# Differences for a seven-product matrix multiplication read back from DRAM as whole rows, and a modulation row moved to PSUM with four loads in flight

## The chip, the core and the metric

The kernel runs on one core of one Trainium2 chip. The metric is the device time of one execution in microseconds (us). Five engines work in parallel, each through its own instruction queue in order: TensorE (PE, with its weight loads as PEld), VectorE (DVE), ScalarE (ACT), GpSimd (POOL) and SyncE (SP), which in this kernel issues every DMA. [...]

## The reference

One layer of a hybrid diffusion backbone over 1024 latent tokens of width 1024, with 256 context tokens. The change touches the two places marked below.

```python
mod_l = (jax.nn.silu(c) @ w_mod[i] + b_mod[i])            # rows 2..5 are "modulation()" in the kernel
sh1, sc1, g1, sh2, sc2, g2 = jnp.split(mod_l, 6, axis=-1)
hl = modulate(rmsnorm(xl, norm1_w[i]), sh1, sc1)          # the normed rows
# token mixer: hl @ w_in is split into SSD input, z, Fourier input, gMLP u and v, and gate logits
g = jax.nn.sigmoid(gate_logits)                           # gate_logits = hl @ w_in[:, OFF_GATE:]
m = g0 * (y_ssd @ w_ssd_o) + g1 * (y_fft @ w_fft_o) + g2 * (y_gmlp @ w_gmlp_o)
xl = xl + g1 * (m @ w_out)
hl2 = modulate(rmsnorm(xl, norm2_w[i]), sh2, sc2)
xl = xl + g2 * conv_ffn(hl2, ...)
return rmsnorm(xl, final_norm_w)
```

## The kernel before

**Number format.** All products are of fp32 data, each operand carried as a high part (fp32r) and a low part that holds the rest: three matmuls (high x high, low x high, high x low) make one product. `hh[k]` and `hl[k]` (k = 0..7, 128 rows x 1024 tokens each) are the high and low part of the modulated, normed latent rows, made in the opening: VectorE scales `xk` in place, ScalarE adds the shift and writes `hh[k]` (L265), VectorE writes `hl[k]` (L266).

**Stages, in order of time.** Opening with the modulation of the first norm (0 to 92 us); projections and the SSD scan (to 545); the v, Fourier and z tiles (to 684); the gates (to 925); the branch products, the output projection and the MLP. A v tile is a projection, a GELU, eight transposes, and a product with `wsT` into `psgm`, which VectorE reads at L750. A z tile (`z_tile`, numbers 4 to 7 here) is 48 matmuls into a PSUM tile `psz`, a tanh on ScalarE (`th`, L649) and a read by VectorE (L650) that frees the PSUM tile. The PSUM pool of the z tiles (two tiles of 1024 columns) is released behind the last z tile, and the gates take its banks in tiles of 512 columns.

**Gates.** 24 blocks of gate logits are made two by two with seven products in place of eight: `gate_unit` and `unit_steps`, with weight combinations from `weight_tools` (`raw` loads `A11`..`A22`, `s_` adds or subtracts, `put` splits into high and low part, L844 to L850) and with operand combinations of four blocks of the normed rows: b11 and b12 are the token halves of rows k, b21 and b22 those of rows k + 4. Needed are t1 = b12 - b11, t2 = b22 - t1, t3 = b22 - b12 and t4 = b21 - b11 - t3, for k = 0..3, each split again into a high and a low part (`split`, L166 and L167). Before, each difference is made from the parts: the low parts subtracted on GpSimd (L1164), the high parts on VectorE (L1166, L1173), then a sum (L1167, L1174), and for t4 one subtraction more (L1180). The tiles come from pool `wx`: tag `rw` with five buffers, which the weight loads `A..` use too, and tag `ws` with three.

**Modulation.** `modulation()` makes the four later modulation rows on VectorE: 64 tensor_tensor_reduce (L1211) of 128 x 512, each on a piece of `w_mod` that SyncE loads into one of the two halves of a tile (`ctanh`), times the SiLU row `crow`, which lies in SBUF. One pair of them is put behind each addition of a gate unit.

**Order.** The code is written in program order; a list scheduler orders each engine's queue by a model of its own, and priorities (`tc.high_priority`) and `tc.issue_after` steer it.

Of the kernel before, what the change touches and what calls it, by code (L numbers as in the profile page):

```python
# [32 lines left out]
def hybrid_block_kernel(ctx: ExitStack, tc: tile.TileContext, a, dbg=None):  # L33
    nc = tc.nc
    V, S, G, PE, SY = nc.vector, nc.scalar, nc.gpsimd, nc.tensor, nc.sync
# [11 lines left out]
    dram = pool("dram", space=bass.MemoryType.DRAM)  # L47
# [4 lines left out]
    def ps_small(name, tag="c"):  # L52
        return pss.tile([P, 512], F32, tag=tag, name=name)
# [105 lines left out]
    def f32(t):  # L159
        return t.bitcast(F32)  # L160
# [34 lines left out]
    for k in range(KT):  # L195
        xk = xT[k // 4][:, k % 4, :]
# [3 lines left out]
        q = s2.tile([P, L], F32, tag="CT", name=f"sqx{k}")  # L200
# [33 lines left out]
    def mod_rows(k):  # L234
# [10 lines left out]
        with tc.high_priority(offset=CHAIN):  # L245
            V.tensor_copy(mrow[k % 2], crow[k % 2])

    hh = [None] * KT
    hl = [None] * KT
    for k in range(KT):  # L250
        mod_rows(k)
        with tc.high_priority(offset=CHAIN):
            for s_ in range(2):
                o = 4 * k + 2 * s_
                PE.matmul(psmod[:, o:o + 2], mrow[k % 2][:, s_ * P:(s_ + 1) * P], sel, start=True, stop=True)
            V.tensor_tensor(mods[:, k], psmod[:, 4 * k:4 * k + 4].rearrange("p (s v) -> p s v", s=2),
                            bc(bmod[:, k:k + 9:8].unsqueeze(2), [P, 2, 2]), op=ALU.add)
            V.scalar_tensor_tensor(mods[:, k, 1], mods[:, k, 1], 1.0, bc(n1w[:, k:k + 1], [P, 2]),
                                   op0=ALU.add, op1=ALU.mult)
        shl, Al, shc, Ac = mods[:, k, 0, 0:1], mods[:, k, 1, 0:1], mods[:, k, 0, 1:2], mods[:, k, 1, 1:2]  # L260
        hh[k] = hpool.tile([P, L], F32R, tag="h", name=f"hh{k}")
        hl[k] = hpool.tile([P, L], F32R, tag="h", name=f"hl{k}")
        xk = xT[k // 4][:, k % 4, :]
        V.scalar_tensor_tensor(xk, xk, Al, rbx, op0=ALU.mult, op1=ALU.mult)
        last_op["hh"] = S.activation(hh[k], xk, AF.Identity, bias=shl)  # L265
        V.scalar_tensor_tensor(hl[k], xk, shl, f32(hh[k]), op0=ALU.add, op1=ALU.subtract)  # L266
        ck = ctxT[k // 4][:, k % 4, :]
        V.scalar_tensor_tensor(ck, ck, Ac, rbc, op0=ALU.mult, op1=ALU.mult)
        S.activation(hch[:, k, :], ck, AF.Identity, bias=shc)
# [373 lines left out]
    def z_tile(g, i, qz):  # L643
        t = 4 * g + i
        wt = win(T_Z + t, f"wz{t}")
        ps = ps_big(f"psz{t}")
        mm3(halves(ps), wt, hx, KT)
        th = tpool.tile([P, L], F32, tag="acc", name=f"th{t}")
        S.activation(th, ps, AF.Tanh, scale=0.5)  # L649
        V.scalar_tensor_tensor(th, th, 1.0, ps, op0=ALU.add, op1=ALU.mult)  # L650
        yv = yacc[g][:, i, :]
        V.tensor_tensor(yv, yv, th, op=ALU.mult)
        if i == 0:
            S.activation(qz, yv, AF.Square)
            return
        q = tpool.tile([P, L], F32, tag="tmp", name=f"yq{t}", bufs=1)
        S.activation(q, yv, AF.Square)
        (G if i % 2 else V).tensor_tensor(qz, qz, q, op=ALU.add)
        if i == 3:
            tok_sums(psq[g], qz, NCH)  # L660
# [49 lines left out]
    for u in (0, 1, 4, 2, 3):  # L710
# [3 lines left out]
        for par, (tt, c0, n) in enumerate(((tpf, 0, NE), (tmf, NE, NO))):  # L714
            ps = ps_small(f"psU{u}{par}", ("c", "c2")[par])
# [52 lines left out]
    HB = 512  # L768
    HS = (slice(0, HB), slice(HB, L))
    ORDER = (1, 6, 5, 7, 2, 3, 4)  # L770
    wx = pool("wx", bufs=2, side="left")
# [381 lines left out]
            h, l = xt[2 * j + k // 2]  # L1153
            Bh[p].append((h[:, k % 2, :], l[:, k % 2, :]))
    for k in range(4):
        b11, b12 = (hh[k][:, HS[0]], hl[k][:, HS[0]]), (hh[k][:, HS[1]], hl[k][:, HS[1]])
        b21, b22 = (hh[k + 4][:, HS[0]], hl[k + 4][:, HS[0]]), (hh[k + 4][:, HS[1]], hl[k + 4][:, HS[1]])

        def tmp(q, tag="rw", n_=5):
            return wx.tile([P, HB], F32, tag=tag, name=f"H{q}{k}", bufs=n_)  # L1160

        def diff(q, x, y):
            o, t = tmp(q), tmp(f"d{q}", "ws", 3)
            G.tensor_tensor(t, f32(x[1]), f32(y[1]), op=ALU.subtract)  # L1164
            with tc.issue_after(last_op["F"].ins):
                V.tensor_tensor(o, f32(x[0]), f32(y[0]), op=ALU.subtract)  # L1166
            V.tensor_tensor(o, o, t, op=ALU.add)  # L1167
            return o

        t1 = diff(1, b12, b11)  # L1170
        t2 = tmp(2)
        with tc.issue_after(last_op["F"].ins):
            V.tensor_tensor(t2, f32(b22[0]), t1, op=ALU.subtract)  # L1173
        V.tensor_tensor(t2, t2, f32(b22[1]), op=ALU.add)  # L1174
        split(t2, *Bh[6][k], V)
        split(t1, *Bh[5][k], G)
        t3 = diff(3, b22, b12)
        split(t3, *Bh[7][k], G)
        t4 = diff(4, b21, b11)
        V.tensor_tensor(t4, t4, t3, op=ALU.subtract)  # L1180
        split(t4, *Bh[4][k], V)

    def gate_unit(b, d, md):
        def consume(r, h, src, spare):
# [14 lines left out]
    def modulation():  # L1199
        cr = tpool.tile([P, D], F32, tag="zz", name="crow", bufs=1)  # L1200
        SY.dma_start(cr, a["crow"].partition_broadcast(P))
        ct = tpool.tile([P, D], F32, tag="tmp", name="ctanh", bufs=1)
        S.activation(ct, cr, AF.Tanh, scale=0.5)
        V.scalar_tensor_tensor(cr, ct, 1.0, cr, op0=ALU.add, op1=ALU.mult)
        wm = ct.rearrange("p (i c) -> p i c", i=2)
        for i in range(2):
            SY.dma_start(wm[:, i], a["wmod1"][0, 0, :, HS[i]])
        for b in range(4):
            for k in range(KT):
                for i in range(2):  # L1210
                    V.tensor_tensor_reduce(out=wm[:, i], in0=wm[:, i], in1=cr[:, HS[i]], scale=0.5, scalar=0.0,  # L1211
                                           op0=ALU.mult, op1=ALU.add, accum_out=mod2[:, i, b, k:k + 1])
                    n_ = b * KT + k + 1
                    if n_ < 4 * KT:
                        SY.dma_start(wm[:, i], a["wmod1"][n_ // KT, n_ % KT, :, HS[i]])
                yield

    y_norm(1, ("y", "y"))
# [518 lines left out]
```

## Time and profile before

| | us |
|---|---|
| median of three runs | 1914.47 (1911.53 to 1917.52) |
| the profiled execution, own time | 1915.69 |
| its span, first to last instruction | 1913.9 |
| PE busy | 1754.1 |
| DVE busy | 1413.0 |
| ACT busy | 849.0 |
| POOL busy | 890.3 |

The profiled execution is 1.2 us above the median of the runs, and its own time 1.8 us above its span. "Busy" is the sum of an engine's instruction times; the idle time in front of an instruction is shown with the engine or DMA that ended it.

### The profile page before, as it was taken

To read this page: it belongs to the slowest core of one execution; us is meant where nothing else is said; L and a number is where in the kernel's file an instruction comes from. 1 tells how busy PE (TensorE), PEld (TensorE's weight loads), DVE (VectorE), ACT (ScalarE), POOL (GpSimd) and SP (SyncE) were. 2 spreads that over 40 slices of the span, in tenths; PEclk is the share of its full clock that TensorE was granted. 3 is DMA by queue.
4 is the path that set the end of the run, shared out by engine and by line. 5 is a ranking of instruction groups with operands and counts; after the bars stand their busy time and mean duration, and the time that the engine had idled before them with its cause. 6 is when DMAs were issued, how large, how long until landed. Compare 5 with 4: busy or idle time off the path is not lost. (4 is left out here: it accounts for less than half of the span.)

```text
span 1913.9 us, 23639 instructions
## 1 busy us (share of the span) xinstructions
PE 1754.1 (92%) x8148; PEld 1409.3 (74%) x8148; DVE 1413.0 (74%) x2002; ACT 849.0 (44%) x1472; POOL 890.3 (47%) x591
## 2 busy tenths in 40 slices
PE   4899998897989879999799999889999999899888
PEld 3688776675668768777687888678888888677677
DVE  7786576786675854666848645899888888968896
ACT  5444355564442334434434234445455545533433
POOL 3222255456542654544655855534343333544543
PEclk9899999999999989999999999899999999899998
DMA  8012365654453124666246463123223224653532
GB/s 331 6 64 67 124 194 145 159 155 116 160 178 105 39 88 165 209 203 217 89 130 207 142 233 131 53 84 109 94 98 133 89 97 167 203 180 113 167 109 89
DMA packets 144608, 260.36 MB, mean 136 GB/s; under 512 B 15452, under 2 KB 56284, under 8 KB 143080
## 3 DMA queue, kind: packets, MB, share of 16 engines
q1 hardware_dynamic: 144488, 258.86, 41.5%
q8 instruction: 64, 1.05, 0.2%
q14 instruction: 56, 0.46, 0.1%
HBM read 205.71 MB, written 53.10 MB: 135 GB/s over the span
## 5 line engine op out<-in xcount | busy, mean ns | idle before, releaser
L1211 DVE CUSTOM_DVE_ANT_0 ctanh<-ctanh,crow 128x512 f32<-128x512 f32 x64 | 57.0, 897 | 41.6 <-DMA ctanh<-in_wmod_dram 41.4
L286 DVE SCALAR_TENSOR_TENSOR acc<-psx,convw,acc 128x1023 f32<-128x1023 f32 (+1 forms) x48 | 61.4, 1279 | 20.0 <-ACT acc L282 19.6
L555 DVE SCALAR_TENSOR_TENSOR rf<-rs,ncuml,rf 128x128 f32<-128x128 f32 x128 | 47.2, 416 | 31.4 <-ACT rf L554 28.9
L1264 POOL TENSOR_TENSOR pwo<-rwo,pwo 128x512 fp32r<-128x512 f32 x32 | 46.9, 1475 | 46.5 <-ACT pwo L1263 43.0
L850 POOL TENSOR_TENSOR w1up<-A11up,w1up 128x512 fp32r<-128x512 f32 x20 | 27.1, 1356 | 88.8 <-ACT w1up L849 79.6
L561 POOL TENSOR_TENSOR rf<-rf,G 128x512 f32<-128x512 f32 x32 | 46.1, 1443 | 45.8 <-DVE G L558 35.5
L850 POOL TENSOR_TENSOR w7up<-S3up,w7up 128x512 fp32r<-128x512 f32 x20 | 29.4, 1472 | 79.9 <-ACT w7up L849 46.2
L558 DVE SCALAR_TENSOR_TENSOR G<-cbm,dtl,G 128x128 f32<-128x128 f32 x128 | 58.6, 517 | 6.0 <-ACT G L557 6.0
L1553 DVE SCALAR_TENSOR_TENSOR xf<-Yd,g,xf 128x512 f32<-128x512 f32 x64 | 46.9, 743 | 11.6 <-PE Yd L860 11.5
L554 ACT ACTIVATE rf<-rf,ncuml 128x128 f32<-128x128 f32 x128 | 41.2, 393 | 31.2 <-DMA rf<-Rd 31.1
L166 ACT ACTIVATE gh<-gr 128x1024 fp32r<-128x1024 f32 (+1 forms) x36 | 37.1, 1034 | 37.5 <-DMA gr<-Gd 36.0
L157 PE MATMUL pso<-mh,pwo 128*128 128x512 f32 x128 | 50.2, 392 | 0.0
L153 PE MATMUL pso<-mh,pwo 128*128 128x512 f32 x128 | 49.8, 390 | 0.0
L155 PE MATMUL pso<-ml,pwo 128*128 128x512 f32 x128 | 49.8, 389 | 0.0
L510 DVE TENSOR_TENSOR scr<-po,ro 128x512 f32<-128x512 f32 x32 | 21.8, 685 | 34.8 <-ACT ro L497 34.6
L497 ACT ACTIVATE ro<-ro 128x512 f32<-128x512 f32 x32 | 20.1, 629 | 58.9 <-DMA ro<-Rd 58.5
L520 PE MATMUL pS<-scr,Bt 128*128 128x512 f32 x56 | 32.1, 658 | 14.4 <-DVE scr L510 13.2
L1469 DVE TENSOR_TENSOR gt<-gt,aa 128x512 f32<-128x512 f32 x44 | 42.9, 974 | 0.1
L557 ACT ACTIVATE G<-cbm,dtl 128x128 f32<-128x128 f32 x128 | 39.7, 391 | 6.4 <-DVE cbm L545 6.4
L850 POOL TENSOR_TENSOR w4up<-A22up,w4up 128x512 fp32r<-128x512 f32 x20 | 31.2, 1559 | 21.2 <-ACT w4up L849 21.2
L1466 ACT ACTIVATE ft<-aa 128x512 f32<-128x512 f32 x44 | 27.8, 631 | 29.5 <-DVE aa L1448 29.5
L522 POOL TENSOR_TENSOR st<-st,etl 128x512 f32<-128x512 f32 x24 | 26.6, 1108 | 29.3 <-DVE st L524 29.3
(1292 smaller groups left out, 6670.4 us busy)
## 6 DMA issues: line engine op xcount, KB each, us to landing
gr<-Gd SPq DMA_DIRECT2D x70, 256.0 KB, 3.4
ctanh<-in_wmod_dram SPq DMA_DIRECT2D x64, 256.0 KB, 3.4
Gd<-gt SPq DMA_DIRECT2D x10, 1536.0 KB, 5.7
wm<-in_wmod_dram SPq DMA_DIRECT2D x16, 512.0 KB, 9.8
ro<-Rd SPq DMA_DIRECT2D x64, 128.0 KB, 3.2
rf<-Rd SPq DMA_DIRECT2D x32, 256.0 KB, 4.6
rs<-Rd SPq DMA_DIRECT2D x32, 256.0 KB, 3.7
sg<-Sg SPq DMA_DIRECT2D x16, 512.0 KB, 3.6
```

Of the source, the lines that this page charges most:

```text
L153: PE.matmul(o, wh[:, k, :], xh[:, sl], start=st, stop=False)
L155: PE.matmul(o, wh[:, k, :], xl[:, sl], start=False, stop=False)
L157: last_op["mm"] = PE.matmul(o, wl[:, k, :], xh[:, sl], start=False, stop=sp)
L286: V.scalar_tensor_tensor(acc[:, lo:hi], ps[:, lo + o:hi + o], cw[:, t, j:j + 1], acc[:, lo:hi], op0=ALU.mult, op1=ALU.add)
L555: V.scalar_tensor_tensor(E[:, h, :], rs[:, h, :], ncum[:, c, 16 + f:17 + f], E[:, h, :], op0=ALU.add, op1=ALU.min)
L558: V.scalar_tensor_tensor(Gm[:, h, :], cbm[:, 1, :], dtl[:, c, 16 + f:17 + f], Gm[:, h, :], op0=ALU.mult, op1=ALU.add)
L561: G.tensor_tensor(E, E, Gm, op=ALU.mult)
L850: (V if p in on_v else G).tensor_tensor(t[:, 1, :], ap, f32(t)[:, 0, :], op=ALU.subtract)
L1211: V.tensor_tensor_reduce(out=wm[:, i], in0=wm[:, i], in1=cr[:, HS[i]], scale=0.5, scalar=0.0, op0=ALU.mult, op1=ALU.add, accum_out=mod2[:, ...
L1264: G.tensor_tensor(t[:, 1, :], raw, f32(t)[:, 0, :], op=ALU.subtract)
L1469: V.tensor_tensor(gt[:, 2 * q + h, :], gt[:, 2 * q + h, :], aa[:, HS[h]], op=ALU.mult)
L1553: V.scalar_tensor_tensor(xv, src, g2[:, dd:dd + 1], xv, op0=ALU.mult, op1=ALU.add)
```

## The change

First, each normed row block is also finished whole: ScalarE adds the shift to `xk` in place (8 more activations of 128 x 1024) and SyncE stores it to a DRAM tile `Hr[k]` (8 stores of 512 KB). Second, the gate operand's blocks are loaded back from there (`blk`, 16 loads of 256 KB into tag `rw`), and each t is one subtraction on VectorE; t4 is b21 - t2, which is the same number, and for k = 2 and 3 it overwrites its block. The four splits of t4 stand behind the last z tile's tanh in the order. Third, the SiLU row of the modulation goes to two PSUM tiles, and the pieces of `w_mod` into four half tiles, so that four loads can be on their way.

```diff
+    Hr = [dram.tile([P, L], F32, name=f"Hr{k}") for k in range(KT)]
...
         V.scalar_tensor_tensor(hl[k], xk, shl, f32(hh[k]), op0=ALU.add, op1=ALU.subtract)
+        raws.append((k, xk, shl))
...
+    for k, xk, shl in raws:
+        S.activation(xk, xk, AF.Identity, bias=shl)
+        with tc.issue_after(last_op["h"].ins):
+            SY.dma_start(Hr[k], xk)
...
-        S.activation(th, ps, AF.Tanh, scale=0.5)
+        last_op["z"] = S.activation(th, ps, AF.Tanh, scale=0.5)
...
-        def diff(q, x, y):
-            o, t = tmp(q), tmp(f"d{q}", "ws", 3)
-            G.tensor_tensor(t, f32(x[1]), f32(y[1]), op=ALU.subtract)
-            with tc.issue_after(last_op["F"].ins):
-                V.tensor_tensor(o, f32(x[0]), f32(y[0]), op=ALU.subtract)
-            V.tensor_tensor(o, o, t, op=ALU.add)
+        def blk(q, kk, h):
+            t = wx.tile([P, HB], F32, tag="rw", name=f"Hb{q}{k}", bufs=5)
+            SY.dma_start(t, Hr[kk][:, HS[h]])
+            return t
+
+        def diff(q, x, y, o=None):
+            o = o if o is not None else wx.tile([P, HB], F32, tag="ws", name=f"H{q}{k}", bufs=3)
+            V.tensor_tensor(o, x, y, op=ALU.subtract)
             return o
 
+        b12, b11, b22 = blk(12, k, 1), blk(11, k, 0), blk(22, k + 4, 1)
         t1 = diff(1, b12, b11)
-        t2 = tmp(2)
-        with tc.issue_after(last_op["F"].ins):
-            V.tensor_tensor(t2, f32(b22[0]), t1, op=ALU.subtract)
-        V.tensor_tensor(t2, t2, f32(b22[1]), op=ALU.add)
+        split(t1, *Bh[5][k], G)
+        t2 = diff(2, b22, t1)
         split(t2, *Bh[6][k], V)
-        split(t1, *Bh[5][k], G)
         t3 = diff(3, b22, b12)
         split(t3, *Bh[7][k], G)
-        t4 = diff(4, b21, b11)
-        V.tensor_tensor(t4, t4, t3, op=ALU.subtract)
-        split(t4, *Bh[4][k], V)
+        b21 = blk(21, k + 4, 0)
+        t4 = diff(4, b21, t2, s1p.tile([P, HB], F32, tag="p1", name=f"H4{k}") if k < 2 else b21)
+        with tc.issue_after(last_op["z"].ins):
+            split(t4, *Bh[4][k], V)
...
-        V.scalar_tensor_tensor(cr, ct, 1.0, cr, op0=ALU.add, op1=ALU.mult)
-        wm = ct.rearrange("p (i c) -> p i c", i=2)
+        crp = [ps_small(f"crp{i}", ("t", "y")[i]) for i in range(2)]
         for i in range(2):
-            SY.dma_start(wm[:, i], a["wmod1"][0, 0, :, HS[i]])
...
+            V.scalar_tensor_tensor(crp[i], ct[:, HS[i]], 1.0, cr[:, HS[i]], op0=ALU.add, op1=ALU.mult)
+        wm = [t[:, HS[i]] for t in (ct, cr) for i in range(2)]
+        todo = [(b, k, i) for b in range(4) for k in range(KT) for i in range(2)]
...
+        for n in range(4):
+            fetch(n)
+        for n, (b, k, i) in enumerate(todo):
+            V.tensor_tensor_reduce(out=wm[n % 4], in0=wm[n % 4], in1=crp[i], scale=0.5, scalar=0.0,
+                                   op0=ALU.mult, op1=ALU.add, accum_out=mod2[:, i, b, k:k + 1])
+            fetch(n + 4)
+            if i == 1:
                 yield
```

Three places show how the queues change. The first is VectorE around the read of z tile 4, before (names: `H21` is t2 of k = 1, `Hd` a difference of low parts, `vt3` the third v tile's read of `psgm`):

```order
L650 SCALAR_TENSOR_TENSOR th4_5006<-th4_5006,psz4_4957 128x1024
L1166 TENSOR_TENSOR H32_5326<-hh6_503,hh2_355 128x512
L1174 TENSOR_TENSOR H22_5319<-H22_5319,hl6_504 128x512
L652 TENSOR_TENSOR yacc1_2677<-yacc1_2677,th4_5006 128x1024
L1167 TENSOR_TENSOR H32_5326<-H32_5326,Hd32_5327 128x512
L167 TENSOR_TENSOR ty1_5251<-H22_5319,tx1_5250 128x512
L1166 TENSOR_TENSOR H42_5333<-hh6_503,hh2_355 128x512
L750 SCALAR_TENSOR_TENSOR vt3_5011<-psgm30_5026,bsb3_4885 128x512
```

The same place in the changed kernel (`Hb122` is the loaded block b12 of k = 2):

```order
L657 SCALAR_TENSOR_TENSOR th4_5030<-th4_5030,psz4_4981 128x1024
L757 SCALAR_TENSOR_TENSOR vt3_5035<-psgm30_5050,bsb3_4909 128x512
L659 TENSOR_TENSOR yacc1_2701<-yacc1_2701,th4_5030 128x1024
L1170 TENSOR_TENSOR H21_5318<-Hb221_5312,H11_5314 128x512
L1170 TENSOR_TENSOR H31_5322<-Hb221_5312,Hb121_5308 128x512
L167 TENSOR_TENSOR ty0_5273<-H21_5318,tx0_5272 128x512
L1170 TENSOR_TENSOR H12_5338<-Hb122_5332,Hb112_5334 128x512
L757 SCALAR_TENSOR_TENSOR vt3_5035<-psgm31_5056,bsb3_4909 128x512
```

The read of `psgm30` moved from seven instructions behind the z tile's read to the one right behind it. The second place is SyncE's queue from the last z tile's weights to the first gate's, which before held only the v tile's load and store between the two:

```order
L137 DMA wz7r_5188<-in_win_dram 128x1024
L1165 DMA Hb122_5332<-Hr2_254 128x512
L752 DMA uT3_5048<-Ud3_585 128x1024
L1165 DMA Hb112_5334<-Hr2_254 128x512
L1165 DMA Hb222_5336<-Hr6_258 128x512
L1165 DMA Hb212_5350<-Hr6_258 128x512
L760 DMA Gm3_3938<-uT3_5048 128x1024
L1165 DMA Hb123_5355<-Hr3_255 128x512
L1165 DMA Hb113_5357<-Hr3_255 128x512
L1165 DMA Hb223_5359<-Hr7_259 128x512
L1165 DMA Hb213_5373<-Hr7_259 128x512
L846 DMA A11g00_5397<-in_win_dram 128x512
```

Eight loads of blocks are new in front of the first gate's weights (`A11g00`), and share their five buffers. The third place is ScalarE in the changed kernel's opening, where L276 is the new activation:

```order
L267 ACTIVATE hh2_363<-xT0_97,mods_249 128x1024
L272 ACTIVATE hch_220<-ctxT0_115,mods_249 128x256
L276 ACTIVATE xT0_97<-xT0_97,mods_249 128x1024
L239 ACTIVATE wmh50_445<-wm50_141 128x1024
L282 ACTIVATE aneg_159<-aneg_159 128x32
L239 ACTIVATE wmh51_457<-wm51_143 128x1024
L267 ACTIVATE hh3_400<-xT0_97,mods_249 128x1024
```

The new activation stands between one block's `hh` and the next blocks' modulation weights (`wmh`), and overwrites what `hl` of its block reads, so that it waits for VectorE.

## Rows read from the trace of the kernel before

**Rows 1.** The page: busy time, share of the span and instructions of each engine.

```profile
PE 1754.1 (92%) x8148; PEld 1409.3 (74%) x8148; DVE 1413.0 (74%) x2002; ACT 849.0 (44%) x1472; POOL 890.3 (47%) x591
```

**Rows 2.** Windows: us, busy PE, PEld, DVE, ACT, POOL, granted clock, DMA share, GB/s.

```profile
50.00:100.00 50.00, 44.29 (x226) 30.97 (x226) 39.39 (x54) 21.97 (x27) 13.23 (x5) 0.90 0.03 11
...
750.00:900.00 150.00, 144.67 (x623) 117.30 (x622) 95.07 (x174) 55.51 (x101) 74.33 (x51) 0.99 0.65 209
900.00:960.00 60.00, 48.34 (x188) 37.10 (x187) 51.62 (x56) 31.84 (x48) 34.27 (x16) 0.93 0.35 119
```

**Rows 3.** Timeline of PE, 545 to 690: start, duration, instruction, idle before and releaser.

```profile
563.61 2.04 PE L700 MATMUL psF<-tabc,fT 128*128 128x128 f32 x8 [4.71 <-DVE tm L707]
...
648.01 2.04 PE L749 MATMUL psgm<-wsT,vt 128*128 128x128 f32 x8 [4.26 <-DVE vt L750]
...
662.79 0.62 PE L153 MATMUL psz<-hh,wz7h 128*128 128x512 f32 x2
...
684.12 0.80 PE L858 MATMUL Yg<-hh,w1g 128*128 128x512 f32 x1 [10.29 <-DVE th L650]
```

**Rows 4.** Windows behind three of these waits, columns as in group 2.

```profile
564.00:570.00 6.00, 6.00 (x23) 5.23 (x23) 3.01 (x4) 3.63 (x4) 1.05 (x1) 0.60 0.38 133
...
648.00:655.00 7.00, 6.99 (x22) 5.90 (x23) 6.86 (x6) 0.63 (x1) 5.71 (x4) 0.56 0.00 0
...
684.00:690.00 6.00, 5.88 (x17) 4.73 (x18) 1.81 (x3) 1.89 (x3) 2.58 (x3) 0.64 0.12 44
```

**Rows 5.** Windows of VectorE with tile H, and of GpSimd with tile Hd.

```profile
575.00:670.00 95.00, 45.07 (x41) 0.96 0.22 73
...
545.00:670.00 125.00, 19.62 (x12) 0.95 0.28 96
```

**Rows 6.** Timeline of VectorE and GpSimd at 553 us, and of VectorE at 708 us.

```profile
553.45 8.82 DVE L668 SCALAR_TENSOR_TENSOR yacc<-yacc,ssdn,rby 128x1024 f32<-128x1024 f32 x4 [0.90 <-ACT rby L185]
...
553.20 3.51 POOL L1164 TENSOR_TENSOR Hd<-hl,hl 128x512 f32<-128x512 f32 x2
...
708.36 1.29 DVE L668 SCALAR_TENSOR_TENSOR yacc<-yacc,ssdn,rby 128x1024 f32<-128x1024 f32 x1 [1.32 <-ACT rby L185]
```

**Rows 7.** Timeline of VectorE and ScalarE, 675 to 684.

```profile
675.13 0.69 DVE L844 TENSOR_TENSOR S1g<-A21g,A22g 128x512 f32<-128x512 f32 x1 [0.81 <-DMA A22g<-in_win_dram]
...
678.68 1.00 ACT L649 ACTIVATE th<-psz 128x1024 f32<-128x1024 f32 x1
...
682.87 1.21 DVE L650 SCALAR_TENSOR_TENSOR th<-th,psz 128x1024 f32<-128x1024 f32 x1
```

**Rows 8.** Lines L1211 and L887: duration ns min/median/max; the first from the page's groups.

```profile
L1211 DVE CUSTOM_DVE_ANT_0 ctanh<-ctanh,crow 128x512 f32<-128x512 f32 x64 | 57.0, 897 | 41.6 <-DMA ctanh<-in_wmod_dram 41.4
...
L1211 DVE CUSTOM_DVE_ANT_0 ctanh<-ctanh,crow x64: 675/693/1817, 745.3 to 903.5; 128x512 f32<-128x512 f32 x64
...
L887 DVE TENSOR_TENSOR Ug<-zg,Ug x12: 678/682/694, 706.3 to 935.4; 128x512 f32<-128x512 f32 x12
...
L887 DVE TENSOR_TENSOR Ug<-Ug,p1g x4: 679/692/1774, 915.6 to 933.6; 128x512 f32<-128x512 f32 x4
```

**Rows 9.** Waits of PE, 750 to 905: total us, times, longest.

```profile
PE Xg L858 <- ACT w2g L849: 3.6, 3, 1.7
```

**Rows 10.** DMA issues: median us to landing, 550 to 680; spread of the ctanh loads.

```profile
A21g<-in_win_dram SPq DMA_DIRECT2D x2, 256.0 KB, 2.5
...
A12g<-in_win_dram SPq DMA_DIRECT2D x1, 256.0 KB, 3.2
...
DMA to landing us min/median/max: 2.6/3.4/6.0
```

**Rows 11.** Timeline of ScalarE in the opening.

```profile
61.06 1.14 ACT L265 ACTIVATE hh<-xT,mods 128x1024 fp32r<-128x1024 f32 x1
```

**Rows 12.** Timeline of GpSimd and PE behind the gates.

```profile
907.27 10.72 POOL L850 TENSOR_TENSOR w3g22b<-S2g22b,w3g22b 128x512 fp32r<-128x512 f32 x1 [3.99 <-ACT w3g22b L849]
...
919.26 0.50 PE L860 MATMUL Xg<-hh,w1g23b 128*128 128x512 f32 x1 [3.53 <-POOL w1g23b L850]
```

More of the change, by code (lines that the diff above doesn't have):

```diff
@@ L246, in mod_rows @@
             V.tensor_copy(mrow[k % 2], crow[k % 2])
+    Hr = [dram.tile([P, L], F32, name=f"Hr{k}") for k in range(KT)]
     hh = [None] * KT
     hl = [None] * KT
+    raws = []
     for k in range(KT):
@@ L1155, in hybrid_block_kernel @@
     for k in range(4):
[L1156 to L1160, printed above, removed]
-        def diff(q, x, y):
-            o, t = tmp(q), tmp(f"d{q}", "ws", 3)
-            G.tensor_tensor(t, f32(x[1]), f32(y[1]), op=ALU.subtract)
-            with tc.issue_after(last_op["F"].ins):
-                V.tensor_tensor(o, f32(x[0]), f32(y[0]), op=ALU.subtract)
-            V.tensor_tensor(o, o, t, op=ALU.add)
+        def blk(q, kk, h):
[5 more added lines that the diff above has]
+            V.tensor_tensor(o, x, y, op=ALU.subtract)
             return o
+        b12, b11, b22 = blk(12, k, 1), blk(11, k, 0), blk(22, k + 4, 1)
         t1 = diff(1, b12, b11)
-        t2 = tmp(2)
-        with tc.issue_after(last_op["F"].ins):
-            V.tensor_tensor(t2, f32(b22[0]), t1, op=ALU.subtract)
-        V.tensor_tensor(t2, t2, f32(b22[1]), op=ALU.add)
+        split(t1, *Bh[5][k], G)
+        t2 = diff(2, b22, t1)
         split(t2, *Bh[6][k], V)
-        split(t1, *Bh[5][k], G)
         t3 = diff(3, b22, b12)
         split(t3, *Bh[7][k], G)
-        t4 = diff(4, b21, b11)
-        V.tensor_tensor(t4, t4, t3, op=ALU.subtract)
-        split(t4, *Bh[4][k], V)
+        b21 = blk(21, k + 4, 0)
+        t4 = diff(4, b21, t2, s1p.tile([P, HB], F32, tag="p1", name=f"H4{k}") if k < 2 else b21)
+        with tc.issue_after(last_op["z"].ins):
+            split(t4, *Bh[4][k], V)
     def gate_unit(b, d, md):
@@ L1203, in modulation, with fetch @@
         S.activation(ct, cr, AF.Tanh, scale=0.5)
-        V.scalar_tensor_tensor(cr, ct, 1.0, cr, op0=ALU.add, op1=ALU.mult)
-        wm = ct.rearrange("p (i c) -> p i c", i=2)
+        crp = [ps_small(f"crp{i}", ("t", "y")[i]) for i in range(2)]
         for i in range(2):
-            SY.dma_start(wm[:, i], a["wmod1"][0, 0, :, HS[i]])
[L1208 to L1215, printed above, removed]
+            V.scalar_tensor_tensor(crp[i], ct[:, HS[i]], 1.0, cr[:, HS[i]], op0=ALU.add, op1=ALU.mult)
+        wm = [t[:, HS[i]] for t in (ct, cr) for i in range(2)]
+        todo = [(b, k, i) for b in range(4) for k in range(KT) for i in range(2)]
+        def fetch(n):
+            if n < len(todo):
+                b, k, i = todo[n]
+                SY.dma_start(wm[n % 4], a["wmod1"][b, k, :, HS[i]])
+        for n in range(4):
[5 more added lines that the diff above has]
+            if i == 1:
                 yield
```

## The prediction

> **What bounds the kernel now.** I read the page's busy shares first: PE works 1754.1 of 1913.9 us [rows 1], so only what PE waits for, or what holds its clock down, can be won or lost; some 160 us of idle are the most that any change off PE could touch. Next the windows along the span, to find idle PE near what the diff touches. Between 50 and 100 us PE is busy 44.29 of 50, from 750 to 900 us 144.67 of 150, and from 900 to 960 us 48.34 of 60 [rows 2]. The rest is in PE's timeline from 545 to 690 us [rows 3]: three waits, 4.71, 4.26 and 10.29 us, each released by VectorE. [...] The work lost there is (1 - 0.60) x 6 = 2.4 us, 0.44 x 7 = 3.1 and 0.36 x 6 = 2.2. The same stretch holds nearly all the work on the differences: VectorE's with tile H take 45.07 us of 95, in 41 instructions, and GpSimd's with tile Hd 19.62 us, in 12 [rows 5]. The sum goes against the profiled execution's own 1915.7 us, which is 1.2 above the median of the runs.
>
> **The opening: 8 activations and 8 stores more.** An activation of 128x1024 takes 1.14 us [rows 11], so 8 x 1.14 = 9.1 us more on ScalarE. Most fall where ScalarE is busy 21.97 of 50 us, and the stores, 8 x 512 KB = 4.2 MB, where the DMA share is 0.03 [rows 2]; that idle time is the cover. But ScalarE's queue is in order: an activation that overwrites xk waits until VectorE has read it for `hl`, and the next block's modulation weights and `hh` stand behind it. VectorE is busy 39.39 of 50, so it does not always come at once. Bounds: -1 (nothing but scatter) and +9.2, all eight on the path. I take +1.0, about one activation exposed, since every block but the last has the idle half of ScalarE around it.
>
> **The first wait (4.71, `psF`).** It hangs on VectorE's chain: the group of L668 that starts at 553.45 takes 8.82 us for four, where the same operation takes 1.29 at 708 us; a difference `Hd` runs on GpSimd beside it, from 553.20 for 3.51 us [rows 6]. Four at 1.29 are 5.2, so 3.6 us were lost beside GpSimd or in its wake. The change takes all 12 `Hd` away; GpSimd keeps splits, and the new loads write SBUF at that time. I take 2.8 of the 4.71, and half of the 2.4 of clock, 1.2: -4.0. Bounds 0 and -7.1.
>
> **The second (4.26, `psgm`).** The read of `psgm` (L750) stands seven instructions behind the z tile's read in VectorE's queue, five of them work on H, and after the change it is right behind it (the first place in the order). Of the 41 rows with tile H, 36 are differences, (45.07 / 41) x 36 = 39.6 us; 16 subtractions take their place at 0.69 [rows 7] to that mean of 1.10, 11 to 18 us, so VectorE has 22 to 29 us more room. I take the whole wait and its 3.1 of clock: -7.4. Bounds -3 and -7.4. A smaller wait of 1 us at 631 us, released likewise, gives -0.5.
>
> **The third (10.29, first gate).** The gate's PSUM banks come free when VectorE has read the last z tile. `th` on ScalarE starts at 678.68, though the tile's matmuls end at 684.12 - 10.29 = 673.83 [rows 3], because the splits of the first gate's weights stand ahead of it, and they wait for `S1g`, added at 675.13 when the load of `A22g` has landed [rows 7]. That load waits for one of the five `rw` buffers, which VectorE frees late. Afterwards the same ring must hand out eight loaded blocks ahead of `A11g` (the second place in the order), so I replayed it from the end of z tile 4. A z tile is 48 matmuls, 673.83 - 662.79 = 11.04 us [rows 3], so the last one's end three tiles later, at 33.1. VectorE's queue from z tile 4's read to the third S of the first gate is 5 operations of 128x1024 at 1.21 and 20 of 128x512 at 0.69: 19.9 us. Three times it waits for a block whose buffer was freed just before, at 2.5 less what stands between, about 2 each: 26. Then `A12g`, 3.2 [rows 10], and the remaining splits on ScalarE, about 3: 32.2. So `th` would be free to start about when the tile ends, with one or two us to spare. The wait then is `th`, 1.00, the read, 1.21 [rows 7], and some 0.3 between: 2.5. The gain is 10.29 - 2.5 = 7.8, and half of the 2.2 of clock, 1.1: -8.9. Bounds 0 (the ring is no faster) and -10. The last two splits of t4, now behind `th`, are 2 x 0.69 on VectorE and needed only by the fifth product of the unit: nothing, unless VectorE is over 10 us behind.
>
> **The modulation.** The 64 reductions take 57.0 us, mean 897 ns, and VectorE waits 41.4 for their loads; the best is 675, the median 693, the worst 1817 [rows 8]. Four loads under way instead of two end most of that idle. With `crow` in PSUM only one operand comes from SBUF, and I read two rows of L887 as a sign that such a form is not slowed by its neighbours: with one PSUM operand it is never above 694 ns, with SBUF operands alone it reaches 1774 [rows 8]. At 0.69 the 64 take 44, 13 us less of VectorE. But PE idles only 150 - 144.67 = 5.33 us there [rows 2], and 3.6 of it is for `Xg` on ScalarE's `w2g` [rows 9], in which VectorE has a part only. I take -3. Bounds 0 and -7 (the 5.33 and a clock of 0.99).
>
> [...]
>
> **Behind the gates, 900 to 960.** PE idles 11.66 us; GpSimd's `w3g22b` takes 10.72 us from 907.27, and PE waits 3.53 at 919.26 for GpSimd [rows 12], while VectorE is busy 51.62 of 60 [rows 2], the remaining reductions among its work. I read the 10.72 us as a wait beside VectorE's work; earlier and shorter reductions thin that work out: -2, bounds 0 and -6 (half the idle).
>
> **The sum.** +1.0 - 4.0 - 0.5 - 7.4 - 8.9 - 3 - 2 = -24.8. 1915.7 - 24.8 = 1890.9, which is 1889.7 against the median; I say 1891.
>
> **The rivals.** *The ring keeps the first gate waiting.* Each round through the five buffers may be no 2.5 us: the `ctanh` loads took 2.6 at least, 3.4 in the median and 6.0 at most [rows 10]. Four rounds at 6.0 are some 14 us later than at 2.5; less the slack of 1 to 2 the wait stays over 10, and the third term's 8.9 goes, with a few us more or less: 1900 to 1903. For it: three or four loads start only when a buffer is freed. Against it: `A21g` in this stretch took 2.5. *The gains are given back behind the gates*, where VectorE is full in any case; half of 24.8 stays: 1902 to 1903. Against it: PE in the gates is busy 96%, and it starts them earlier. *More comes back*: every wait and all the clock behind it, -7.1 - 1.0 - 7.4 - 10 - 7 - 5 = -37.5: 1878. *Slower: the opening.* Each new activation waits for VectorE's `hl`, and the next block's `hh` and the matmuls on it behind that; with 3.2 us for each of eight blocks on the path, 26 us, the gain of 25.8 elsewhere is gone, and that is the point from which it decides. At 4 us each it gives 1922. For it: VectorE is busy 79% in that window. Against it: ScalarE idles 28 of 50 us there, and the activations stand after a block's other work. *The parts don't do what they say*: loads from DRAM and PSUM operand slower than counted, so that VectorE has as much to do as before: within 0.3%. The reductions would have to take 2 us each for it.
>
> **Chances and range.** My forecast 0.58, its own range 1882 to 1899 (bounds of the terms, not all at once); the ring 0.17; given back 0.08; more 0.09; no change 0.04; slower 0.04. A measurement of this kernel tells 0.3%, 5.7 us, from no change: faster is below 1908.7. From the cases: the forecast, the ring, given back and more are nearly all below it, less a tail of 0.09 of the four: faster 0.83, same 0.10, slower 0.07. The range of 1878 to 1907 takes in the ring, giving back and half of the more; outside are some 0.2.
>
> **What would show it.** Right: the wait at `psgm` gone, VectorE's read of it right behind the z tile's read; the first `Yg` of the first gate waits 2 to 3 us on `th`; the window behind it at a clock over 0.8; the `psF` wait under 2.5; the reductions all near 0.69 with DMA idle before them under 10 us; PE in the window 50 to 100 within 1 us of 44.29. Wrong: a first gate that waits for `w1g` or `w2g` with A loads landing after z tile 7's end; PE idle growing in the opening, with a wait on `hh`; a new PE wait behind the gates as long as what was won before.

## The result and the profile after

The changed kernel takes 1888.72 us, the median of 4 runs (1883.76 to 1893.05), against 1913.57 for the kernel before; the ratio is 0.9867 with a 95% interval of 0.9837 to 0.9896, so some 25 us less, 20 to 31 by the interval. The forecast was 1891 us. The time came out as predicted, but two terms of the sum were wrong by several us each, in opposite directions, and that is what this part is about.

The profiled execution is the one of 1883.76 us, 5.0 below the median, so places are compared in the trace and totals by the medians. First the page: busy time and instructions of each engine, and then, as in [rows 2], windows with busy time of PE, PEld, DVE, ACT and POOL, the granted clock, the DMA share and GB/s.

```profile
PE 1747.4 (93%) x8148; PEld 1409.2 (75%) x8148; DVE 1383.9 (74%) x1983; ACT 859.9 (46%) x1480; POOL 856.0 (45%) x579
```

```profile
50.00:100.00 50.00, 44.45 (x236) 31.78 (x235) 41.27 (x58) 29.67 (x35) 14.60 (x5) 0.93 0.22 85
750.00:900.00 150.00, 150.00 (x663) 124.16 (x662) 96.47 (x189) 67.20 (x114) 75.75 (x54) 1.00 0.63 205
900.00:960.00 60.00, 53.70 (x227) 43.11 (x226) 46.77 (x46) 27.36 (x44) 33.04 (x21) 0.97 0.37 125
```

PE has the same 8148 instructions and is 6.7 us shorter at them. In the opening it is as busy as before. In the gates (750 to 900 us) it no longer idles at all. Next PE's timeline around the waits of [rows 3]. The waits of 4.26 us at the v tile and of 0.99 us have no row any more; these two are left:

```profile
563.79 1.33 PE L707 MATMUL psF<-tabc,fT 128*128 128x128 f32 x8 [2.76 <-DVE tm L714]
...
672.42 0.79 PE L865 MATMUL Yg<-hh,w1g 128*128 128x512 f32 x1 [7.80 <-DVE th L657]
```

The same places in both traces, by the start of the named instruction of PE, give the time line of the gain (a table made from rows of the two traces):

| place | before, us | after, us | difference |
|---|---|---|---|
| `rby` of the first norm (L183) | 544.68 | 546.70 | +2.0 |
| last `psF` group | 563.61 | 563.79 | +0.2 |
| first gate, `Yg` | 684.12 | 672.42 | -11.7 |
| convolution behind the gates, first `pa` | 1017.3 | 987.6 | -29.7 |
| end of the span | 1913.9 | 1882.0 | -31.9 |

The first row measures no cost of the change, since it lies within the scatter between executions: in six more kernels of this document whose code is the changed kernel's up to there, the same instruction starts between 544.23 and 548.94 us. The stretch behind the convolution's start scatters too, from 892.8 to 898.6 us in these kernels. So a place is best compared by the time from one row to another.

So 13.7 us come back between `rby` and the first gate, where the prediction had 20.8, 5.4 of them clock, and 18.0 from the first gate to the convolution, where it had 5. This last stretch holds the same 1340 matmuls before (first fence) and after (second); the columns are those of the windows above:

```profile
684.12:1017.30 333.18, 315.83 (x1340) 255.13 (x1340) 202.53 (x303) 132.22 (x225) 171.44 (x111) 0.97 0.49 159
```

```profile
672.42:987.60 315.18, 308.02 (x1340) 252.69 (x1340) 199.81 (x308) 135.63 (x227) 162.01 (x112) 0.99 0.52 171
```

Idle PE fell from 17.35 to 7.16 us, 10.2 less, and busy PE from 315.83 to 308.02, 7.8 less, for the same matmuls: that part is clock, 0.97 to 0.99 over the stretch. In the gates themselves 211.38 us became 202.48 (to 895.5 and to 874.9 us, 887 and 888 matmuls), 8.9 less, and the part behind them, up to the convolution, is 9.1 shorter. The reductions of [rows 8] are now (page's groups; in the last column what VectorE waited for):

```profile
L1220 DVE CUSTOM_DVE_ANT_0 ctanh<-ctanh,crp 128x512 f32<-128x512 f32 x32 | 20.9, 682 | 4.1 <-DMA ctanh<-in_wmod_dram 4.1
L1220 DVE CUSTOM_DVE_ANT_0 crow<-crow,crp 128x512 f32<-128x512 f32 x32 | 20.7, 680 | 0.1
```

41.6 us in place of 57.0, and 4.1 us of waiting in place of 41.4, as forecast. What was not forecast stands in VectorE's timeline ahead of the first gate (start, duration, idle before and releaser):

```profile
643.96 5.18 DVE L1170 TENSOR_TENSOR H<-Hb,H 128x512 f32<-128x512 f32 x3
...
655.92 2.89 DVE L1170 TENSOR_TENSOR H<-Hb,Hb 128x512 f32<-128x512 f32 x1
658.74 1.78 DVE L1170 TENSOR_TENSOR Hb<-Hb,H 128x512 f32<-128x512 f32 x1
660.44 1.78 DVE L167 TENSOR_TENSOR ty<-H,tx 128x512 fp32r<-128x512 f32 x1
```

and beside them on GpSimd:

```profile
645.15 2.84 POOL L139 TENSOR_TENSOR wz7l<-wz7r,wz7h 128x1024 fp32r<-128x1024 f32 x1
...
655.47 2.80 POOL L665 TENSOR_TENSOR qz<-qz,yq 128x1024 f32<-128x1024 f32 x1
658.23 1.74 POOL L857 TENSOR_TENSOR w1g<-A11g,w1g 128x512 fp32r<-128x512 f32 x1
659.92 1.75 POOL L167 TENSOR_TENSOR ty<-H,tx 128x512 fp32r<-128x512 f32 x1
```

The subtractions that my replay (the third wait of the prediction) set at 0.69 us each take up to 2.89 while GpSimd has an instruction of its own under way.

### The profile page after: what moved, and what is told of

The parts are those of the page before. It is cut to its first block, busy times and chain, and to the rows that moved or that the text cites. A ratio compares the mean times of both kernels' runs of the same rounds, so it can differ in the third digit from the quotient of the medians.

```text
span 1882.0 us, 23647 instructions
## 1 busy us (share of the span) xinstructions
PE 1747.4 (93%) x8148; PEld 1409.2 (75%) x8148; DVE 1383.9 (74%) x1983; ACT 859.9 (46%) x1480; POOL 856.0 (45%) x579
## 5 line engine op out<-in xcount | busy, mean ns | idle before, releaser
L562 DVE SCALAR_TENSOR_TENSOR rf<-rs,ncuml,rf 128x128 f32<-128x128 f32 x128 | 52.2, 454 | 32.4 <-ACT rf L561 29.2
L527 PE MATMUL pS<-scr,Bt 128*128 128x512 f32 x56 | 32.9, 671 | 15.4 <-DVE scr L517 12.0
L167 DVE TENSOR_TENSOR gl<-gr,gh 128x1024 fp32r<-128x1024 f32 (+1 forms) x26 | 39.7, 1527 | 4.2 <-ACT gh L166 3.6
```

What stands on the lines that cost most here:

```text
L562: V.scalar_tensor_tensor(E[:, h, :], rs[:, h, :], ncum[:, c, 16 + f:17 + f], E[:, h, :], op0=ALU.add, op1=ALU.min)
```

## The experiments

Differences in us below are (ratio - 1) times the median of the kernel before in the same comparison (1914.8, 1915.4 and 1914.8 us), with the interval of the ratio. The three questions: which part carries the gain, what in the modulation does it, and what the first gate still waits for.

**Modulation alone.** The kernel before, with `modulation()` of the changed kernel:

```diff
-            V.tensor_tensor_reduce(out=wm[:, i], in0=wm[:, i], in1=cr[:, HS[i]], ...
+            V.tensor_tensor_reduce(out=wm[n % 4], in0=wm[n % 4], in1=crp[i], ...
+            fetch(n + 4)
```

> The kernel before with the modulation part of the change alone (row in PSUM, four loads). Theory A, the prediction's own split: the parts F and G, -5 us, so 1908 to 1910, with the first gate's wait near 10 us as before and PE idle in 750 to 900 us under 2 us. Theory B, read from the place where the two traces part (first gate to the convolution, some -18 us): the modulation carries more than half of the gain, -12 to -18, 1896 to 1902. Both expect all 64 reductions near 0.69 us and under 10 us of VectorE waiting on their loads.

Measured 1900.60 us, ratio 0.9928 (0.9906 to 0.9949), -13.8 us (-18.0 to -9.8). Theory B. From the first gate to the convolution the window is

```profile
687.17:1002.00 314.83, 307.92 (x1340) 253.16 (x1340) 190.02 (x303) 135.19 (x225) 159.83 (x111) 0.98 0.52 169
```

within half a us of the changed kernel's 315.18, in idle and in busy time of PE. The first gate waits 10.82 us here, as before. So the 18 us of this stretch belong to the modulation part; the total shows 13.8 of them, and its interval just takes in 18.

**Differences alone.** The changed kernel with the old `modulation()`, that is, the edit above the other way round.

> The changed kernel with the old modulation (row in SBUF, two loads), so stored rows and new differences alone. Theory A: -24.8 + 5 = -20 us, 1893 to 1896, with psgm's wait gone and the first gate waiting under 4 us. Theory B: only what the trace had won up to the first gate, -10 to -12 us, 1901 to 1904; the first gate waits 6 to 9 us for the last z tile's read, and the reductions are at a mean near 0.9 us again.

Measured 1900.42 us, ratio 0.9917 (0.9896 to 0.9937), -15.9 us (-19.9 to -12.1). The gain lies between those of the two theories, and its interval just leaves out both; by the time itself theory B's 1901 is nearer. The signs are those of theory B: the first gate waits 7.80 us (6 to 9 expected), and the reductions are back at a mean of 937 ns. The stretch behind it is as long as in the kernel before, 335.15 against 333.18:

```profile
671.45:1006.60 335.15, 316.13 (x1340) 255.50 (x1340) 211.92 (x308) 132.90 (x227) 172.66 (x112) 0.97 0.50 161
```

The two parts add up to -29.7 where both together gave -25; the intervals don't tell that from a plain sum.

**Opening alone.** The kernel before with the activations and the stores, nobody reading them:

```diff
+    for k, xk, shl in raws:
+        S.activation(xk, xk, AF.Identity, bias=shl)
+        with tc.issue_after(last_op["h"].ins):
+            SY.dma_start(Hr[k], xk)
```

> The kernel before with the eight activations and eight stores alone, the stored rows not read. Prediction: +1.0 us, bounds -1 to +9.2. Theory C, from the markers (PE 2.0 us later at 545 us after the change): +2, 1915 to 1916. The rival that ends slower: each block's hh late by its wait, +8 or more, 1922, and then PE idle must grow between 50 and 100 us from 5.7 us to 10 or more.

Measured 1917.97 us, ratio 1.0019 (1.0004 to 1.0033), +3.6 us (+0.8 to +6.3). The +1.0 of the prediction lies inside, near its lower end. No stall shows between 50 and 100 us, where PE is busy 44.50:

```profile
50.00:100.00 50.00, 44.50 (x236) 31.78 (x236) 41.01 (x59) 30.39 (x36) 14.60 (x5) 0.93 0.21 85
```

Where the 3.6 us lie was not found: this trace reaches `rby` at 547.08 us, inside the scatter named above, and its execution, 1915.91 us, is 2.1 below the median of the run.

**Two loads, row in PSUM.** Apart from the number of loads this is the changed kernel:

```diff
-        wm = [t[:, HS[i]] for t in (ct, cr) for i in range(2)]
+        wm = [ct[:, HS[i]] for i in range(2)]
...
-            fetch(n + 4)
+            fetch(n + 2)
```

> The changed kernel with two loads under way in place of four, the row still in PSUM. Theory L (the number of loads is what matters): VectorE's waits on the loads are 30 us or more as before, and the time is that of the kernel with the old modulation within 2 us. Theory O (the operand matters, because the slowed reductions held VectorE): the reductions are near 0.69 us, and the time is within 2 us of the changed kernel, 1887 to 1891, in spite of the waits on the loads.

Measured 1890.51 us, ratio 0.9877 (0.9852 to 0.9903). Theory O by the medians: this one is 1.8 us above the changed kernel's and 9.9 below that of the kernel with the old modulation, while VectorE waits as long for its loads as before (groups of lines):

```profile
L1220 DVE CUSTOM_DVE_ANT_0 ctanh<-ctanh,crp 128x512 f32<-128x512 f32 x64 | 43.6, 686 | 45.4 <-DMA ctanh<-in_wmod_dram 45.2
```

So bringing the slowed reductions back to 0.69 us is worth most of it. The stretch from the first gate to the convolution tells more than the medians:

```profile
669.22:990.60 321.38, 310.33 (x1340) 253.22 (x1340) 196.24 (x309) 133.62 (x227) 166.88 (x112) 0.98 0.52 168
```

It is 13.8 us shorter than with the old modulation (335.15), but 6.2 longer than in the changed kernel (315.18), 0.9 of that in the gates and 5.3 behind them. With the row in PSUM and four loads this stretch takes 314.2 to 317.0 us in seven kernels of this document, and with the row in SBUF and two loads 330.3 to 335.2 in four. So in the traces ending VectorE's waits on the loads is worth some 4 to 7 us, though only one execution of this kernel was traced, and its total, 1.8 us above the changed kernel with runs from 1887 to 1903, does not tell it from nothing.

**Result in PSUM, inputs in SBUF.** Old modulation, two loads, but the product goes to a PSUM tile:

```diff
-                    V.tensor_tensor_reduce(out=wm[:, i], in0=wm[:, i], in1=cr[:, HS[i]], ...
+                    V.tensor_tensor_reduce(out=crp[i], in0=wm[:, i], in1=cr[:, HS[i]], ...
```

> The changed kernel with the old modulation, both inputs of the reduction in SBUF and two loads, but the elementwise result written to PSUM. Theory P (two SBUF inputs are what is slowed): reductions up to 1.8 us with a mean near 0.9, time that of the kernel with the old modulation, 1898 to 1903. Theory W (any third SBUF stream, the write too, is what is slowed): all reductions near 0.69 us and 1888 to 1892.

Measured 1903.13 us, ratio 0.9940 (0.9913 to 0.9967). Theory P: it is the second input in SBUF, not the traffic of the result (mean 902 ns with the result in PSUM, 937 with it in SBUF in the differences-alone run, 897 before). The line's spread (duration in ns, minimum, median, maximum, and first and last start) is close to that of the kernel before, and the stretch from the first gate to the convolution takes 332.59 us:

```profile
L1214 DVE CUSTOM_DVE_ANT_0 crp<-ctanh,crow x64: 682/701/1751, 736.5 to 894.4; 128x512 f32<-128x512 f32 x64
```

**Almost no reductions.** 60 of the 64 and their loads are left out, and the rows filled with zeros:

```diff
+            if n < 4:
-            V.tensor_tensor_reduce(out=wm[n % 4], ...
-            fetch(n + 4)
+                V.tensor_tensor_reduce(out=wm[n % 4], ...
```

> The changed kernel with 60 of the 64 reductions and their loads left out (the later modulation rows are zero there). If the change has taken all that the modulation cost: within 3 us of the changed kernel, 1886 to 1890, since PE has no idle in the gates there. If VectorE's 41 us still cost something behind the gates: 5 us or more less, 1880 to 1884, with PE's wait for Ug there (3.5 us) gone.

Measured 1886.67 us, ratio 0.9857 (0.9832 to 0.9882), 2.1 us below the changed kernel's median, inside both intervals. The stretch from the first gate to the convolution takes 315.72 us against 315.18, and PE's wait for `Ug` is still there (3.3 us). In the changed kernel the modulation costs nothing more that can be measured.

**t1 and t2 in PSUM.** For k = 2 and 3, the ones made in front of the first gate, t1 and t2 are written to PSUM, so that t2, t4 and two splits have one input there:

```diff
-        t1 = diff(1, b12, b11)
-        split(t1, *Bh[5][k], G)
-        t2 = diff(2, b22, t1)
+        pt = [ps_small(f"H{q}{k}", ("t", "y")[q - 1]) if k > 1 else None for q in (1, 2)]
+        t1 = diff(1, b12, b11, pt[0])
+        split(t1, *Bh[5][k], V if k > 1 else G)
+        t2 = diff(2, b22, t1, pt[1])
```

> The changed kernel with t1 and t2 of k = 2 and 3 written to PSUM and both split by VectorE (t1's split leaves GpSimd). Theory C (the first gate waits because subtractions with two SBUF operands run at 1.1 to 2.9 us beside GpSimd): those with an operand in PSUM take 0.69, the third S of the first gate comes 3 to 5 us earlier against z tile 7's end, and the gate's wait falls from 7.8 us to 3 to 5; 3 to 6 us less than the changed kernel, 1883 to 1886. Theory R (the first gate waits for a buffer): the wait stays within 1.5 us of 7.8.

Measured 1883.25 us, ratio 0.9828 (0.9802 to 0.9853), -32.9 us (-37.9 to -28.2): theory C. The line of the subtractions in the changed kernel (first fence) and in this one (second; durations in ns, minimum, median, maximum):

```profile
L1170 DVE TENSOR_TENSOR H<-Hb,Hb x8: 679/694/2894, 568.2 to 655.9; 128x512 f32<-128x512 f32 x8
L1170 DVE TENSOR_TENSOR H<-Hb,H x6: 677/1235/2880, 568.9 to 654.2; 128x512 f32<-128x512 f32 x6
L1170 DVE TENSOR_TENSOR Hb<-Hb,H x2: 677/1228/1779, 649.7 to 658.7; 128x512 f32<-128x512 f32 x2
```

```profile
L1170 DVE TENSOR_TENSOR H<-Hb,Hb x8: 679/697/2868, 565.7 to 650.7; 128x512 f32<-128x512 f32 x8
L1170 DVE TENSOR_TENSOR H<-Hb,H x6: 677/680/692, 566.4 to 653.1; 128x512 f32<-128x512 f32 x6
L1170 DVE TENSOR_TENSOR Hb<-Hb,H x2: 671/674/677, 650.1 to 655.0; 128x512 f32<-128x512 f32 x2
```

The form with both inputs in SBUF still reaches 2.87 us; t2 and t4 of k = 2 and 3, which now read PSUM, are at 0.69 or under, though for only two of these four (at 653.08 and 655.03 us) GpSimd was at work beside them. The other four of the six `H<-Hb,H`, t2 and t4 of k = 0 and 1, still read SBUF and are short because GpSimd is idle beside them in this run, so a part of the gain is a shift in time and not the place of an input. The edit also takes two splits off GpSimd, so that the place of the input and the work beside it were not separated here. The third S of the first gate starts at 658.57, 3.6 us ahead of z tile 7's end; in the changed kernel it is 663.78 and 0.8 us, so 2.7 us were won, a little under the 3 to 5 expected. The first gate's wait falls, from 7.80 us to 5.00:

```profile
667.15 0.69 PE L865 MATMUL Yg<-hh,w1g 128*128 128x512 f32 x1 [5.00 <-DVE th L657]
```

By the medians this kernel is 5.5 us under the changed one; the two intervals of the ratios overlap by a little, so it is probably, not certainly, the faster. From `rby` to the convolution its trace is 2.4 us shorter (438.5 against 440.9), about what the wait lost; the rest of the 5.5 is not accounted for.

**Late t4.** The loads of b21 and t4 for k = 2 and 3 stand behind the first gate's weight loads, which frees two of the five buffers; t4 is made from the two parts of t2:

```diff
+        def fourth(k=k):
+            b21 = blk(21, k + 4, 0, k)
+            t4 = diff(4, b21, f32(Bh[6][k][0]), b21)
+            V.tensor_tensor(t4, t4, f32(Bh[6][k][1]), op=ALU.subtract)
...
+        if nm == "g00":
+            for f in late:
+                f()
```

> The changed kernel with the loads of b21 and the t4 of k = 2 and 3 moved behind the first gate's weight loads, so that two of the five buffers are no longer held until the last z tile's split; t4 is made there as b21 less the two parts of t2, two subtractions more. Theory R (buffer): A12 of the first gate is loaded 2 us or more earlier against z tile 7's end and the gate's wait falls from 7.8 to 5 or less, 1884 to 1887. Theory C (slowed VectorE): the wait stays within 1.5 us of 7.8, time as the changed kernel.

Measured 1891.15 us, ratio 0.9876 (0.9851 to 0.9900). The wait did not fall, it grew:

```profile
676.13 0.79 PE L865 MATMUL Yg<-hh,w1g 128*128 128x512 f32 x1 [10.71 <-DVE th L657]
```

The buffer did come earlier, as theory R asks: SyncE issues the load of `A12g` 7.6 us ahead of z tile 7's end (657.82 against 665.42), in the changed kernel 0.1 ahead (664.50 against 664.62). So the ring by itself is not what holds the gate. But theory C's figure for the wait was off too. The moved subtractions and the two extra ones stand on VectorE ahead of the product that z tile 6's square on ScalarE waits for (5.67 us), and the last tanh stands behind that square: it starts at 673.82.

**Tanh ahead of the splits.** The last z tile's tanh is put ahead of three weight splits and of z tile 6's square in ScalarE's order, first in the changed kernel, then together with t1 and t2 in PSUM:

```diff
+            with tc.issue_after(last_op["z"].ins):
+                w[2] = put(2, a12)
+                w[7] = put(7, s3_)
+                w[4] = put(4, a22)
...
+        if t == 6:
+            pend.append(square)
+            return
```

> The changed kernel with the last z tile's tanh ahead of the splits w2g, w7g and w4g of the first gate and of the square of z tile 6 in ScalarE's order; VectorE's subtractions as they are. If the splits ahead of the tanh are what the first gate still waits for: the wait falls from 7.8 us to 3 to 5 and the time by 3 to 5 us, 1884 to 1886. If VectorE's lateness alone decides (the read stands behind the sum that waits for A12g): the wait stays over 6 us and the time within 2 us of the changed kernel.

> The same order together with t1 and t2 of k = 2 and 3 in PSUM. Both causes taken away: the first gate's wait falls to the 2.5 to 3.5 us that tanh and read take, 2 us less than with t1 and t2 in PSUM alone, 1880 to 1882. If the order is worth nothing: the wait stays near 5 us and the time near 1883.

Alone: 1883.54 us, ratio 0.9840 (0.9811 to 0.9869), the wait 6.12 us. The time is the one expected of a cure, the wait the one expected of none, so the run tells less than it should; the wait fell by 1.7 us, and the other 3 or so of the time are not accounted for; its interval overlaps that of the changed kernel. In its trace the last tanh is done by 665.5 us, but VectorE reads it at 668.72 only, behind the sum that waits for `A12g`, as the second case had it. Together: 1886.33 us, ratio 0.9846 (0.9821 to 0.9870), and the wait is down to

```profile
669.26 0.50 PE L875 MATMUL Yg<-hh,w1g 128*128 128x512 f32 x1 [2.40 <-DVE th L659]
```

which is the 2.5 us that the prediction had worked out, tanh plus read. But the total did not follow: z tile 7's matmuls end at 666.86, against 667.15 - 5.00 = 662.15 with PSUM alone, and the convolution starts 2.0 us later than there. That lateness is older than the gate: the first matmul of the first z tile starts at 362.7 us against 359.6, ahead of anything that the edit moves, and `rby` at 550.43 against 544.23. From `rby` to the convolution this trace is 4.2 us shorter than with PSUM alone (434.3 against 438.5); behind that it is 8.8 longer (901.6 against 892.8), far from the splits and the square that the edit moves. So two causes of the gate's wait are shown, VectorE's lateness and ScalarE's order, and removing the second pays as far as the convolution in this one trace; that the total gains by it is not shown.

**The opening's additions on GpSimd**, on top of t1 and t2 in PSUM:

```diff
-        S.activation(xk, xk, AF.Identity, bias=shl)
+        G.tensor_scalar(xk, xk, shl, None, op0=ALU.add)
```

> t1 and t2 of k = 2 and 3 in PSUM, and the eight additions of the shift in the opening made by GpSimd in place of ScalarE. If the activations on ScalarE hold the opening (the stores and activations alone came out 3.6 us slower, 1917.97 against 1914.83): 2 to 4 us less than the same kernel with ScalarE's, 1879 to 1881. If that difference is noise or comes from the stores: 1882 to 1885.

Measured 1891.07 us, ratio 0.9875 (0.9851 to 0.9898), 7.8 us above the same kernel with ScalarE's. Neither case came true. On GpSimd six of the eight in-place additions take 3.01 to 4.07 us and the other two 8.82 together, on ScalarE each 1.13 to 1.15, and the modulation weights' low parts (`wml`) queue behind it, so that PE is busy 38.46 of 50 us (GpSimd's timeline, then the window):

```profile
45.56 8.82 POOL L276 TENSOR_SCALAR xT<-xT,mods 128x1024 f32<-128x1024 f32 x2 [1.19 <-DVE hl L268]
54.34 3.25 POOL L240 TENSOR_TENSOR wml<-wm,wmh 128x1024 fp32r<-128x1024 f32 x1
```

```profile
50.00:100.00 50.00, 38.46 (x195) 25.85 (x193) 37.47 (x47) 19.78 (x24) 34.97 (x13) 0.90 0.19 75
```

This is a relative of the prediction's slow rival, with the additions in front of `wml` on GpSimd in place of `hh` on ScalarE: 6 us of PE in one window from an addition in the wrong queue.

## Why the prediction was right, and where it was not

**Opening, +1.0.** Right in mechanism: PE stands at 44.45 against 44.29 of 50 us, so ScalarE's idle time covered the activations there. The size may be low (+0.8 to +6.3 measured, at a place that was not found).

**First wait, -4.0.** The chain of four is 6.97 us (8.82 in [rows 6]), and the wait 2.76 instead of 4.71: -1.95 against the -2.8 taken, and just over the 2.5 named as the sign of being right. The split `wv3l` stayed on GpSimd beside the chain, and the 1.29 that I priced the four at was among the shortest of the line's eight rows before (last fence: minimum, median, maximum). The clock behind it is 0.72 (0.60 in [rows 4]), (0.72 - 0.60) x 6 = 0.7 us against 1.2. The 2.4, 3.1 and 2.2 us of clock in the three terms are estimates of this kind, (1 - granted clock) times the length of the windows of [rows 4].

```profile
555.48 6.97 DVE L675 SCALAR_TENSOR_TENSOR yacc<-yacc,ssdn,rby 128x1024 f32<-128x1024 f32 x4 [0.92 <-ACT rby L185]
...
557.71 2.46 POOL L139 TENSOR_TENSOR wv3l<-wv3r,wv3h 128x1024 fp32r<-128x1024 f32 x1 [3.89 <-issue]
```

```profile
L668 DVE SCALAR_TENSOR_TENSOR yacc<-yacc,ssdn,rby x8: 1271/2208/3364, 553.5 to 713.6; 128x1024 f32<-128x1024 f32 x8
```

**Second wait, -7.4, and the small one, -0.5.** Right: both gone, and the clock from 648 to 655 us is 1.00 with PE full. VectorE's read of `psgm` (634.95) stands right behind the z tile's read (633.82).

**Third wait, -8.9.** Wrong in size. It went from 10.29 to 7.80, and the clock behind it stayed down (0.60 from 672.4 to 678.4 us; the gate's matmuls of 128x512 start 0.43 us apart from 673.0 to 676.9 and 0.23 from 677.5 on), so the term was some -2.5. The step that failed is "5 operations of 128x1024 at 1.21 and 20 of 128x512 at 0.69: 19.9 us": I set the subtractions at their best duration, though the mean of the old ones, 45.07 / 41 = 1.10 [rows 5], was in my hands and used as a bound one paragraph earlier. From z tile 4's read to the end of the third S VectorE was busy 28.24 us with these 25 operations (window, busy VectorE); at 1.10 the 20 would have made it 28.1.

```profile
633.82:664.46 30.64, 28.24 (x26) 1.00 0.36 129
```

Five operations of 128x512 between 652 and 662 us took 1.15, 1.78, 2.89, 1.78 and 1.78, together 9.4 us for 3.45. The read of z tile 4 itself starts 4.1 us behind that tile's matmuls, a lag that the replay put at nothing. The waits for blocks were shorter than taken (2.4 us idle in that window against 6), and `A12g` and the splits behind it took 5.7 of the 6.2 expected. So the last tanh starts at 670.11, 5.5 us behind z tile 7's end in place of one ahead. The ring of buffers, the rival that also left the gate waiting, had the symptom right and the cause wrong: `A12g` did land late (667.06, 2.4 us behind z tile 7's end), but its buffer was late because VectorE was. The late-t4 run frees two buffers and the wait grows; the PSUM run leaves the buffers as they are and the wait falls to 5.0.

What the runs show is that these VectorE instructions with two inputs in SBUF get longer where GpSimd works beside them: the subtractions of 128x512 took 0.68 to 0.69 us with GpSimd idle and up to 2.89 beside it. With one input in PSUM the 64 reductions stayed at 691 ns at most, against 1817 with both in SBUF. What in GpSimd's work slows them was not shown. The prediction saw the sign of it in L887 and used it for the modulation, but not for the subtractions.

**Modulation, -3, and behind the gates, -2.** Right in mechanism, mis-sized: together -13.8 us as a part of its own, and -18 in the trace's stretch, beyond the two bounds together (-7 and -6). By place it is -8.9 in the gates for -3, and -9.1 behind them for -2. The failing step is the bound, "the 5.33 and a clock of 0.99" and "half the idle": I counted PE's idle time from 750 to 900 us and half of that behind, and nearly no clock. The same 1340 matmuls were 7.8 us longer before, and 10.2 of the 17.35 us of idle went. The second half of the stated mechanism, the row in PSUM, was worth most of it, some 10 us by the medians and 14 in the stretch; the first half, four loads that end VectorE's waits, 6.2 us in the stretch of one trace and 1.8 by the medians, which is not clear of noise. The input in PSUM shows no price of its own: the 64 reductions took 675 ns at their best and 693 in the median before, and all of them 670 to 691 after.

**The sum.** Some 7 us too much ahead of the gates (20.8 for 13.7) and 9 to 13 too little behind their start (5 for 13.8 to 18); that -24.8 met -25 is in good part luck. Whether the slowed VectorE or the GpSimd splits beside it held PE in the gates was not separated: GpSimd's 112 instructions of the stretch also take 162.01 us in the changed kernel and 172.66 with the old modulation.

## What to carry to other kernels

Where VectorE and GpSimd work at the same time, don't price a VectorE operation of two SBUF inputs by its shortest row but by its mean or maximum in that stretch (0.69 us with GpSimd idle and up to 2.89 beside it for the subtractions here), and see whether one input can lie in PSUM: for these reductions that was worth about 10 us, and doubling the loads in flight some 6 in one trace and nothing that the total could tell. A long wait of VectorE for a DMA may be worth far less than its length (some 6 us of PE's time for 45 here); look for what the slowed operations delay. To value PE's small waits, compare PE's busy time over the same matmuls in two traces, since the clock behind them can be nearly as much as the idle time itself (7.8 us beside 10.2 here). And compare executions from one row to another, not by the clock time of a row, since the code ahead of it may run some us longer or shorter each time.

## What the runs showed of the hardware that was not expected

A reduction of 128x512 with both inputs in SBUF took up to 1817 ns, with its result in PSUM up to 1751, and with one input in PSUM never over 691: the place of the result made no difference (mean 902 ns against 897 and 937), that of one input did (681). A subtraction of 128x512 with both inputs in SBUF that takes 0.69 us while GpSimd is idle took 1.15, 1.78 or 2.89 beside it. An addition of a column to 128x1024 in place was 1.13 to 1.15 us on ScalarE; on GpSimd six of eight took 3.01 to 4.07 and the other two 8.82 together. And with the same code up to there `rby` started between 544.23 and 548.94 us in seven traces, so that a wait shortened by 2.6 us (tanh first, PSUM) can be seen from row to row and be lost in the total of one execution.
